# A two-layer hybrid decoder step on one core: plain products where the halves are still apart, mixtures made behind them, and two PSUM readers changed

## The chip, the core and the metric

The kernel runs on one core of a Trainium2 chip. The metric is device time in microseconds, the median over several executions. A core has five engines that run side by side, each with its own queue in order: TensorE (PE, matrix products and transposes, with its weight loads shown as PEld), VectorE (DVE), ScalarE (ACT), GpSimd (POOL) and SyncE (SP), which here issues the DMAs. Products land in PSUM; DVE and ACT read it.

## The reference

One inference step for a prompt of 1024 tokens and 8 single sample tokens, model width 1024, two layers:

```python
# layer 0: sliding-window attention, 32 query heads on 4 key/value heads of 64, window 128
q, k, v, g = split(rmsnorm(x) @ w_in_attn)
logits = where(valid, q k^T / 8 + rel_bias, -1e30)     # 128 newest keys of each query
p = exp(logits - m);  w = p / (sum(p) + exp(sink - m))
x = x + (silu(g) * (w @ v)) @ w_out_attn
# layer 1: retention, 4 heads, 256 wide keys, 512 wide values, chunks of 128
q, k, v, g = split(rmsnorm(x) @ w_in_ret);  q, k = rotary(q), rotary(k) / 16
o = ((q k^T) * decay) @ v + (q @ R) * cross;   R = decay^128 * R + (k * decay)^T @ v
x = x + (silu(g) * groupnorm(o)) @ w_out_ret
y = rmsnorm(x)
```

Also returned are the last window of keys and values and the retention states, for prompt and samples. All inputs are float32.

## The kernel before

**Numbers.** Every large float32 operand is split into a high part (a cast to the engine's `fp32r` format) and a low part (the difference). A product is three matmuls: high x high, high x low, low x high. The split of a weight tile (`wsplit`, L200 to L202) is one cast on ACT and one subtraction on POOL or DVE.

**Halves and quarters.** The 1032 tokens are two halves: half 0 has 512 prompt tokens and the 8 samples, half 1 the other 512. A half is two quarters, QT = 256 and QS = 264 columns. The activations stand transposed, with the model width over partitions in 8 blocks of 128. Blocks k and k + 4 are handled as a pair, so that with the two quarters each half is a 2 x 2 arrangement of blocks: a1, a2 (block k) and b1, b2 (block k + 4).

**Mixed jobs.** The input projections use a scheme with seven block products in place of eight. `mixtures(h, k, f)` makes, besides the plain parts of a1 (index 0), b1 (1) and b2 (6), four mixtures: sums and differences of the four blocks (indices 2 to 5). `part` writes the high and low part of one index. `mixed(wa, wb)` makes the seven weight tiles from four loaded ones by differences (`minus`, L230). `unit_job` runs seven products of 12 matmuls for each half that it handles, and adds up the results out of PSUM on DVE (`plus`, L430). A unit is two output tiles of 128 columns.

**Order.** TensorE's order is written out by hand: a `Stream` of jobs, each a generator that yields after a product, and `spread`, which calls other stages between the steps. A weight tile is prepared one tile ahead, and loaded up to three tiles before that. The other engines' instructions are ordered by the framework's planner, which also picks buffers from each pool (a tag names a group of `bufs` buffers).

**Start.** `first_load` brings pair k of a half. `first_pair` squares both blocks for the norm (ACT; summed on DVE at L289), multiplies by the gain (L1125) and calls `mixtures`. The first jobs run on one half at a time: values of half 0 (`v_unit(0)`), keys of half 0 (`k_unit(0)`), values of half 1, a turning of the values of half 0, keys of half 1, the other turning. Then come eight query and eight gate units of both halves, among which the attention stages are spread.

**Attention.** For each of 64 tiles (128 queries, 4 heads): `att_scores`, then `att_turn` transposes the probabilities into PSUM (`pt`). It makes `ptc`, the keys of the same block, as a product with a mask on DVE (L753), and `ptp`, those of the block before, by a copy on ACT (L757) and a selection on POOL (L758). `att_values` multiplies both with the values (L775). `ptc` and `ptp` have one buffer each.

**Layer boundary.** `norm(h)` makes the normalised blocks of layer 1 (L1149) and calls `mixtures`. As half 0 is ready before half 1, the two gate units (`rg_unit`) and two value units (`rv_unit`) of retention head 0 are run on half 0, then on half 1, each as a mixed job of one half; then two rotary units of both halves.

**Retention.** A chunk of 128 tokens: `ret_scores` (scores and turned keys in one PSUM tile `skt`; from it `scf`, its parts `sch` and `scl`, and the decayed keys' parts `kth` and `ktl`), `ret_turn_v`, `ret_values` (output `ro` in PSUM, state update `rp`), `group_norm` (statistics on DVE from `ro`, a power on POOL, and the scaling on ACT, L908, from `ro` into `on`), and `ret_turn`, which transposes `on` (`oT`). The PSUM tiles `skt`, `vtp`, `ro`, `oT`, `pt`, `o` and those of the sample stages share two buffers (tag `w`). In SBUF, `on`, the two tiles of the rotation and a few short rows share three (tag `s`).

Of the kernel before, what the change touches and what calls it, by code (L numbers as in the profile page):

```python
# [19 lines left out]
P = 128  # L20
# [106 lines left out]
def hybrid_step(ctx: ExitStack, tc: tile.TileContext, I: dict, O: dict):  # L127
# [171 lines left out]
    def new_h(h):  # L299
        H[h] = [[None] * 4 for _ in range(7)]  # L300

    def part(h, c, k, src, eng):

        if k % 2 == 0:
            HC[h, c, k // 2] = [htile(h, c, k // 2, n, [P, 2, QS], F32R, f"h{h}{c}{n}") for n in "hl"]
        w = src.shape[-1]
        hh, hl = [t[:, k % 2, :w] for t in HC[h, c, k // 2]]
        act.copy(hh, src)
        eng.tensor_tensor(out=hl, in0=src, in1=r32(hh), op=ALU.subtract)
        H[h][c][k] = (hh, hl)  # L310

    def mixtures(h, k, f):


        a1, a2 = f[:, 0, 0:QS], f[:, 0, QS : 2 * QS]
        b1, b2 = f[:, 1, 0:QT], f[:, 1, QS : 2 * QS]
        part(h, 0, k, a1, pool)
        part(h, 1, k, b1, vec)
        part(h, 6, k, b2, vec)
        vec.tensor_tensor(out=b2, in0=a2, in1=b2, op=ALU.add)  # L320
        pool.tensor_tensor(out=a2, in0=a1, in1=a2, op=ALU.subtract)
        vec.tensor_tensor(out=a1, in0=b2, in1=a1, op=ALU.subtract)
        part(h, 2, k, a1, vec)
        part(h, 3, k, b2, pool)
        part(h, 4, k, a2, vec)
        vec.tensor_tensor(out=b1, in0=b1, in1=a1[:, 0:QT], op=ALU.subtract)
        part(h, 5, k, b1, pool)
# [138 lines left out]

    def spill(dr, halves=(0, 1), tell=None):

        h0, nh = halves[0], len(halves)

        def done(f, q, x, psum):
            if psum:
                t = ctile(q, nh)
                act.copy(t, x)
                x = t
            if tell is not None:
                tell(f, q, x)
            sp.dma_start(dr[:, f, h0 : h0 + nh, span(q)], x)

        return done  # L480
# [76 lines left out]
    sink = cp.tile([P, HEADS], F32, name="sink")  # L557
    sink2 = cp.tile([P, HEADS], F32, name="sink2")
    nsink2 = cp.tile([P, HEADS], F32, name="nsink2")
    sink_s = cp.tile([16, 4], F32, name="sink_s")  # L560
    nsink_s = cp.tile([16, 4], F32, name="nsink_s")
# [3 lines left out]
    def bias_rows():  # L565
# [9 lines left out]
        rb = cp.tile([NBUCKET, HEADS], F32, name="rb")  # L575
# [20 lines left out]
    def k_unit(h):  # L596
        def tell(f, q, x):
# [4 lines left out]
            elif q:  # L602
                ksmp[f] = cp.tile([P, NB], F32, name=f"ksmp{f}")
                vec.tensor_copy(ksmp[f], x[:, 0, QT:QS])

        unit_job(I["w_in0"][16], I["w_in0"][17], spill(kdram, (h,), tell), (h,))
# [14 lines left out]
    def v_unit(h):  # L621
# [3 lines left out]
        def done(f, q, x, psum):  # L625
# [3 lines left out]
            act.copy(d[:, f, span(q)], x[:, 0])  # L629
# [20 lines left out]
        unit_job(I["w_in0"][18], I["w_in0"][19], done, (h,))  # L650
# [95 lines left out]
    def att_turn(i):  # L746
# [8 lines left out]
        if not first:  # L755
            ptp = lp.tile([P, 4, P], F32, name="ptp", tag="ptp", bufs=1)
            act.copy(ptp, pt)  # L757
            pool.affine_select(out=ptp, in_=ptp, pattern=[[0, 4], [-1, P]], base=-1, channel_multiplier=1, compare_op=ALU.is_ge, fill=0.0)  # L758
# [79 lines left out]
    def rg_unit(u, t, halves=(0, 1)):  # L838
        f = 32 + 4 * u + 2 * t
        unit_job(I["w_in1"][f], I["w_in1"][f + 1], spill(rgd[u][t], halves), halves)  # L840

    def rv_unit(u, t, halves=(0, 1)):
        f = 16 + 4 * u + 2 * t
        unit_job(I["w_in1"][f], I["w_in1"][f + 1], spill(rvd[u][t], halves), halves)
# [44 lines left out]
    def group_norm(o, c2, cc):  # L889
# [14 lines left out]
        on = ap_.tile([P, 512], F32, name="on", tag="s", bufs=SB)[:n]  # L904
        if cc is None:
            vec.tensor_scalar(out=on, in0=o, scalar1=r[:, 0:1], scalar2=r[:, 1:2], op0=ALU.mult, op1=ALU.add)
        else:
            act.activation(on, o, AF.Identity, bias=r[:, 1:2], scale=r[:, 0:1])  # L908
# [18 lines left out]
    def ret_scores(u, gc):  # L927
# [11 lines left out]
        vec.scalar_tensor_tensor(out=sf, in0=w[:, 0:P], scalar=kd, in1=m_le, op0=ALU.mult, op1=ALU.mult)  # L939
        sh = lp.tile([P, P], F32R, name="sch", tag="sch", bufs=1)  # L940
# [3 lines left out]
        kth = lp.tile([P, 256], F32R, name="kth", tag="kth", bufs=1)  # L944
        act.activation(kth, w[:, P : 3 * P], AF.Copy, scale=kd)
        ktl = lp.tile([P, 256], F32R, name="ktl", tag="ktl", bufs=1)
        vec.scalar_tensor_tensor(out=ktl, in0=w[:, P : 3 * P], scalar=kd, in1=r32(kth), op0=ALU.mult, op1=ALU.subtract)
# [21 lines left out]
    def ret_values(u, gc):  # L969
# [10 lines left out]
        else:  # L980
            R = lp.tile([P, 2, 512], F32, name="R", tag="R", bufs=1)
        if gc == 0:
# [8 lines left out]
        CH["on", u, gc] = group_norm(o, cst[:, C_C2 + 8 * u + gc : C_C2 + 8 * u + gc + 1], cst[:, C_CC + 8 * u + gc : C_CC + 8 * u + gc + 1])  # L991
# [12 lines left out]
    def ret_sample(u):  # L1004
# [12 lines left out]
        yield  # L1017
        tt = [sm.tile([P, 2, NB], F32, name="rrt", tag="rrt", bufs=2) for _ in range(2)]
# [9 lines left out]
        def load(i):  # L1028
            Rs, vs = [], []
            for b in (2 * i, 2 * i + 1):  # L1030
# [3 lines left out]
                for dt in range(2):  # L1034
                    R = lp.tile([P, 512], F32, name="Rsm", tag="Rsm", bufs=4)
# [76 lines left out]
    def first_load(h, k):  # L1112
        f = X0[h, k] = big("x0")
        zeros(f, h)
        src = I[f"x{h}"][k : KT : 4].rearrange("a p t -> p a t")
        sp.dma_start(f[:, :, 0:QT], src[:, :, 0:QT])
        sp.dma_start(f[:, :, QS : QS + real(h) - QT], src[:, :, QT : real(h)])

    def first_pair(h, k):
        f = X0.pop((h, k))  # L1120
        for j in range(2):
            square(f[:, j, :], 2 * QS, sums.setdefault(h, []))
        for j in range(2):
            kt = k + 4 * j
            vec.tensor_scalar(out=f[:, j, :], in0=f[:, j, :], scalar1=gcol[:, 0, kt : kt + 1], scalar2=None, op0=ALU.mult)  # L1125
        mixtures(h, k, f)
# [8 lines left out]
    def norm(h):  # L1135
# [19 lines left out]
        new_h(h)  # L1155
        for k in range(4):
            mixtures(h, k, fs[k])
# [19 lines left out]

    stream.todo[0].load()
    first_load(0, 0)
    first_load(0, 1)  # L1180
    stream.todo[1].load()
    first_load(0, 2)
    first_load(0, 3)
    stream.todo[2].load()
    for k in range(4):
        first_pair(0, k)
    sp.dma_start(cst, I["cst"])
    stream.ahead = AHEAD
    first_load(1, 0)
    first_load(1, 1)  # L1190
    bias = bias_rows()
    st = [stager(first_stats(h)) for h in range(2)]

    def pair_b(k):
        first_pair(1, k)
        if k < 2:
            first_load(1, k + 2)

    for f in (nothing, nothing, nothing, st[0], st[0], lambda: pair_b(0), lambda: next(bias), lambda: pair_b(1),
              nothing, lambda: pair_b(2), lambda: next(bias), lambda: pair_b(3)):  # L1200
        stream.step()
        f()
    stream.finish(1)
    stream.step()
    st[1]()
    stream.step()
    st[1]()
    sums.clear()
    stream.finish(4)
# [87 lines left out]
    for u in range(RH):  # L1297
        if u:
            n_head.append(jobs(rg_unit, u, 0) + jobs(rg_unit, u, 1))
        else:  # L1300
            n_b = [jobs(f, 0, t, (h,)) for h in range(2) for f in (rg_unit, rv_unit) for t in range(2)]
            n_head.append(0)
        n_head[-1] += jobs(rot_unit, 2 * u, rqd[u]) + jobs(rot_unit, 8 + 2 * u, rkd[u])
        if u:
            n_head[-1] += jobs(rv_unit, u, 0) + jobs(rv_unit, u, 1)
# [12 lines left out]
    spread(4, [stager(norm(1))] * 8 + [nothing] * 2)  # L1318
    stream.finish(4)
# [36 lines left out]
    for u in range(1, RH):  # L1356
        sm_ = [stager(ret_sample(u - 1))] * 22
# [14 lines left out]
    spread(outs1[1], mix([stager(load_y(1, 2))] * 9, chunks(29, 33), [sm_] * 12))  # L1372
# [117 lines left out]
```

## Time and profile before

| | us |
|---|---|
| median of 3 runs | 1898.75 (1896.29 to 1898.92) |
| profiled execution | 1893.53 |
| its span, first to last instruction | 1891.7 |
| PE busy | 1684.4 (89%) |
| DVE busy | 1203.1 (64%) |
| POOL busy | 915.8 (48%) |
| ACT busy | 838.9 (44%) |

Busy time is the union of an engine's instructions. A matmul's recorded duration is longer than the distance to the next one, as they overlap; where PE runs without a pause, the distance is what counts. In the rows, "L202" is a line of the kernel, "out<-in" the tiles, "x13" the count, then busy time in us and mean ns of one, and after a second bar the idle time in front of these instructions with what ended it. In a row of waits stand the waiting instruction, the one that released it, the us in total, the number of waits and the longest. A row of stretches lists, for each engine, the busy us and in brackets the instructions, then the share of its clock that TensorE was granted, and the DMA share and rate.

### The profile page before, as it was taken

How to read it: one execution, taken by the hardware profiler on the slowest of the kernel's cores; microseconds unless marked ns; L12 is line 12 of the kernel's file. 1: busy time of each engine (PE TensorE's matmuls, PEld its weight loads, DVE VectorE, ACT ScalarE, POOL GpSimd, SP SyncE). 2: the span in 40 equal slices, each digit the busy share in tenths (PEclk: the TensorE clock that was granted, in tenths of full speed). 3: DMA queues.
4: the chain of work that ended last, by engine and by line, in shares of the span. 5: the costliest groups of instructions: out<-in, count | busy, mean ns of one | idle time of the engine just before them, and what ended most of it. 6: DMA issues, size and time to landing. Idle time of an engine off the chain costs nothing. (4 is left out here: it accounts for less than half of the span.)

```text
span 1891.7 us, 32933 instructions
## 1 busy us (share of the span) xinstructions
PE 1684.4 (89%) x12072; PEld 1502.3 (79%) x12072; DVE 1203.1 (64%) x2075; ACT 838.9 (44%) x1927; POOL 915.8 (48%) x769
## 2 busy tenths in 40 slices
PE   5699998999998999987789899989998989699996
PEld 3589887788887777866789889878988879677885
DVE  7944665767667776577753676557646764767446
ACT  5544554555555454434443344334434444343223
POOL 6664454655545442335774544444544544434212
PEclk6799999999999999989899999999999999999997
DMA  4434434343435631433245565466537557664324
GB/s 141 114 116 151 147 119 127 99 130 113 126 105 174 225 106 63 154 94 103 77 135 169 169 207 168 127 201 207 175 124 217 204 189 231 219 201 140 107 68 134
DMA packets 211170, 277.99 MB, mean 147 GB/s; under 512 B 32936, under 2 KB 122656, under 8 KB 211008
## 3 DMA queue, kind: packets, MB, share of 16 engines
q1 hardware_dynamic: 211008, 275.88, 46.0%
q8 instruction: 95, 1.56, 0.3%
q14 instruction: 67, 0.55, 0.1%
HBM read 185.46 MB, written 92.42 MB: 147 GB/s over the span
## 5 line engine op out<-in xcount | busy, mean ns | idle before, releaser
L202 POOL TENSOR_TENSOR wlo<-wraw,whi 128x512 fp32r<-128x512 f32 x240 | 331.7, 1383 | 400.9 <-ACT whi L200 385.1
L200 ACT CAST whi<-wraw 128x512 fp32r<-128x512 f32 x432 | 265.3, 616 | 455.9 <-PE gemm L425 229.6
L540 PE MATMUL gemm<-yh,whi 128*128 128x260 f32 (+2 forms) x800 | 262.2, 328 | 13.9 <-DVE xf L548 13.6
L542 PE MATMUL gemm<-yh,wlo 128*128 128x260 f32 (+2 forms) x800 | 255.3, 319 | 0.0
L541 PE MATMUL gemm<-yl,whi 128*128 128x260 f32 (+2 forms) x800 | 254.4, 318 | 0.0
L202 DVE TENSOR_TENSOR wlo<-wraw,whi 128x512 fp32r<-128x512 f32 x192 | 166.3, 866 | 110.4 <-ACT whi L200 108.3
L540 PEld LDWEIGHTS gemm<-yh,whi 128*128 128x128 f32 x800 | 154.3, 193 | 37.3 <-issue 16.9
L230 POOL TENSOR_TENSOR wraw<-wraw 128x512 f32<-128x512 f32 x96 | 148.5, 1551 | 49.3 <-DVE wraw L230 35.8
L430 DVE TENSOR_TENSOR cq<-cq,gemm 128x512 f32<-128x512 f32 (+1 forms) x144 | 89.4, 621 | 119.5 <-PE gemm L426 79.8
L696 ACT ACTIVATE L<-L,nm 128x128 f32<-128x128 f32 x256 | 99.8, 391 | 144.0 <-DVE nm L691 140.1
L542 PEld LDWEIGHTS gemm<-yh,wlo 128*128 128x128 f32 x800 | 153.7, 192 | 10.1
L541 PEld LDWEIGHTS gemm<-yl,whi 128*128 128x128 f32 x800 | 154.2, 193 | 9.0
L700 POOL TENSOR_TENSOR L<-L,rsum 128x512 f32<-128x512 f32 x64 | 72.7, 1136 | 151.8 <-DVE rsum L699 65.7
L230 DVE TENSOR_TENSOR wraw<-wraw 128x512 f32<-128x512 f32 x96 | 91.0, 948 | 20.1 <-POOL wlo L202 17.0
L1054 DVE SCALAR_TENSOR_TENSOR Rsm<-vrow,ksm,Rsm 128x512 f32<-128x512 f32 x64 | 59.0, 951 | 27.3 <-ACT Rsm L1053 17.7
L545 DVE TENSOR_TENSOR xf<-xf,gemm 128x520 f32<-128x520 f32 x64 | 44.3, 692 | 48.9 <-PE gemm L542 48.8
L548 DVE TENSOR_TENSOR xf<-xf,gemm 128x512 f32<-128x512 f32 (+1 forms) x72 | 44.7, 622 | 47.3 <-PE gemm L542 47.2
L509 POOL TENSOR_TENSOR yl<-yf,yh 128x520 fp32r<-128x520 f32 (+1 forms) x32 | 44.0, 1374 | 60.8 <-ACT yh L508 60.8
L733 PE MATMUL S<-kk,q 64*128 64x256 f32 (+1 forms) x512 | 69.2, 389 | 0.1
L424 PE MATMUL gemm<-h06h,whi 128*128 128x264 f32 x168 | 52.1, 310 | 16.2 <-DVE cq L430 16.2
L677 POOL TENSOR_TENSOR g<-g,RB 128x1040 f32<-128x1040 f32 (+1 forms) x16 | 38.5, 2404 | 57.7 <-DMA g<-gd 49.7
L953 POOL TENSOR_TENSOR ql<-qk,qh 128x256 fp32r<-128x256 f32 x28 | 25.1, 897 | 84.9 <-ACT qh L951 61.6
(358 smaller groups left out, 5748.0 us busy)
## 6 DMA issues: line engine op xcount, KB each, us to landing
wraw<-in_w_in SPq DMA_DIRECT2D x192, 256.0 KB
wraw<-in_w_out SPq DMA_DIRECT2D x96, 256.0 KB
ydram<-y SPq DMA_DIRECT2D x32, 512.0 KB
Rsm<-in_state SPq DMA_DIRECT2D x64, 256.0 KB
out_ret_state_sample<-Rsm SPq DMA_DIRECT2D x64, 256.0 KB
yf<-ydram SPq DMA_DIRECT2D x32, 260.0 KB
yf<-ydram SPq DMA_DIRECT2D x32, 256.0 KB
v<-rv SPq DMA_DIRECT2D x32, 256.0 KB
```

The costliest lines, as they stand in the source:

```text
L200: act.copy(hi, raw)
L202: eng.tensor_tensor(out=lo, in0=raw, in1=r32(hi), op=ALU.subtract)
L230: eng.tensor_tensor(out=out, in0=x, in1=y, op=ALU.subtract)
L424: pe.matmul(o, wh, hh, start=(first and k == 0), stop=False, skip_group_check=not first)
L430: vec.tensor_tensor(out=x, in0=x, in1=ps, op=ALU.add)
L540: pe.matmul(ps, a, yh[:, c0:c1], start=(k == 0), stop=False)
L541: pe.matmul(ps, a, yl[:, c0:c1], start=False, stop=False)
L542: pe.matmul(ps, b, yh[:, c0:c1], start=False, stop=(k == 3))
L696: act.activation(L[:, i, :], L[:, i, :], AF.Exp, bias=nm[:, i : i + 1], accum_out=rs[:, i : i + 1])
L700: pool.tensor_tensor(out=L, in0=L, in1=rs[:, :, None].to_broadcast([n, nh, P]), op=ALU.mult)
L733: pe.matmul(S[:, 2 * par + j, w0:256], q[r, j, cs], kk[r, (gb - 1) * P + w0 : (gb + 1) * P], start=True, stop=True)
L1054: vec.scalar_tensor_tensor(out=R, in0=vs[j // 2], scalar=ksm[:, dt, b : b + 1], in1=R, op0=ALU.mult, op1=ALU.add)
```

## The change

1. **Plain jobs.** `plain_job` runs all eight block products of one half: four weight tiles as they are loaded, 96 matmuls, sums kept in PSUM, one copy out per result. Keys and values of both halves and the two gate units of retention head 0 use it. It needs a fourth plain part, of a2 (index 7), whose parts get buffers that are free at that time (`home`).
2. **Value units of head 0** are run on both halves at once, as mixed jobs, after the rotary units.
3. **`mixtures` is split** into `plain_parts` (four plain parts) and `mixture` (the four mixed ones), and the calls are moved: plain parts first, mixtures between later steps. At the start the plain parts come straight from the loaded block with the gain folded in: the high part by an ACT activation with a scale, the low part by a DVE instruction for each. Squares and the gain on the whole block follow. `first_load` takes one block in place of two. In layer 1, block 0's and block 1's low parts are on DVE, those of 6 and 7 on POOL.
4. **`ptp`** is `pt - ptc`, one DVE instruction.
5. **`ret_scores`** issues `kth` and `ktl` ahead of `sch` and `scl`. **`ret_values`** copies `ro` to SBUF on ACT (`on`), and the group norm reads and scales that copy in place.
6. The sample generator of retention has one more empty stage; small tiles move to other pools, and `Rsm` is a little larger.

```diff
-    def mixtures(h, k, f):
-        a1, a2 = f[:, 0, 0:QS], f[:, 0, QS : 2 * QS]
-        b1, b2 = f[:, 1, 0:QT], f[:, 1, QS : 2 * QS]
-        part(h, 0, k, a1, pool)
-        part(h, 1, k, b1, vec)
-        part(h, 6, k, b2, vec)
+    def plain_parts(h, k, j, f, home, gains=None):
+        a, b = parts(f)[2 * j : 2 * j + 2]
+        g = None if gains is None else gains(k + 4 * j)
+        part(h, j, k, a, vec, g)
+        if j:
+            part(h, 6, k, b, pool, g)
+        else:
+            part(h, 7, k, b[:, 0 : QT if h else QS], pool, g, home)
+    def mixture(h, k, f):
+        a1, a2, b1, b2 = parts(f)
...
+            act.activation(hh, src, AF.Copy, scale=gain)
+            vec.scalar_tensor_tensor(out=hl, in0=src, scalar=gain, in1=r32(hh), op0=ALU.mult, op1=ALU.subtract)
...
+    def plain_job(wa, wb, done, h):
+        def run():
+            hs = H[h]
+            gs = [gtile(), gtile()]
+            ns = [QT, QT if h else QS]
+            for z in range(2):
+                for f in range(2):
+                    hi, lo = stream.tile()
+                    for q, n in enumerate(ns):
+                        o = gs[f][:, q, :n]
+                        for k in range(4):
+                            hh, hl = [x[:, :n] for x in hs[(0, 7, 1, 6)[2 * z + q]][k]]
+                            wh, wl = hi[:, k * P : (k + 1) * P], lo[:, k * P : (k + 1) * P]
+                            pe.matmul(o, wh, hh, start=(z == 0 and k == 0), stop=False)
+                            pe.matmul(o, wh, hl, start=False, stop=False)
+                            pe.matmul(o, wl, hh, start=False, stop=(z == 1 and k == 3))
+                    if z:
+                        for q, n in enumerate(ns):
+                            done(f, q, gs[f][:, q : q + 1, :n], True)
+                    yield 24 * mm_ns(QS)
...
-            act.copy(ptp, pt)
-            pool.affine_select(out=ptp, in_=ptp, pattern=[[0, 4], [-1, P]], base=-1, channel_multiplier=1, compare_op=ALU.is_ge, fill=0.0)
+            vec.tensor_tensor(out=ptp, in0=pt, in1=ptc, op=ALU.subtract)
...
+        on = ap_.tile([P, 512], F32, name="on", tag="s", bufs=SB)
+        act.copy(on, o)
...
-        CH["on", u, gc] = group_norm(o, ...)
+        CH["on", u, gc] = group_norm(on, ...)
...
     for k in range(4):
-        first_pair(0, k)
+        first_load(0, k, 0)
+        stream.todo[k].load()
+    for k in range(4):
+        first_load(0, k, 1)
+    first_parts(0, 0)
+    stream.step()
+    stream.ahead = AHEAD
+    first_parts(0, 1)
+    stream.step()
     sp.dma_start(cst, I["cst"])
+    first_squares(0, 0)
+    stream.step()
...
+    first_squares(0, 1)
+    stream.finish(1)
...
+    for k in range(4):
+        stream.step()
+        if k < 2:
+            st[0]()
+        mixture(0, k, X0[0, k])
...
-    spread(4, [stager(norm(1))] * 8 + [nothing] * 2)
-    stream.finish(4)
+    nb = stager(norm(1))
+    spread(2, [nb] * 6 + [na] * 2)
+    spread(2, [nb] * 4)
     stream.finish(n_head[0])
```

176 lines of the change are left out of this document (108 added, 68 removed).

## The prediction

> **What bounds the kernel now.** I read the totals first, then a table of busy time over stretches that I cut at the kernel's own stages, then TensorE's waits (PE) stage by stage, then the costliest lines of the other engines inside the stages where PE waits. PE is busy 89% of the span, so the question is where the rest lies.
>
> ```profile
> PE 1684.4 (89%) x12072; PEld 1502.3 (79%) x12072; DVE 1203.1 (64%) x2075; ACT 838.9 (44%) x1927; POOL 915.8 (48%) x769
> ```
>
> The cuts come from the first matmul of the first two-half job of layer 0 (118.08), the first matmul of layer 1 (881.21) and the first two-half job of layer 1 (1000.38):
>
> ```profile
> 118.08 0.57 PE L424 MATMUL gemm<-h00h,whi 128*128 128x264 f32 x1
> ```
> ```profile
> 881.21 0.57 PE L424 MATMUL gemm<-h00h,whi 128*128 128x264 f32 x1
> ```
> ```profile
> 1000.38 0.29 PE L424 MATMUL gemm<-h00h,whi 128*128 128x264 f32 x1
> ```
> ```profile
> core 0: us, PE busy (x) PEld busy (x) DVE busy (x) ACT busy (x) POOL busy (x), PEclk, DMA share, GB/s
> 7.70:118.00 110.30, 66.92 (x381) 57.35 (x381) 91.28 (x147) 57.98 (x135) 75.08 (x65) 0.75 0.40 116
> 118.00:700.00 582.00, 548.22 (x4231) 474.83 (x4231) 375.96 (x728) 292.39 (x826) 297.43 (x244) 0.98 0.43 136
> 700.00:881.00 181.00, 166.08 (x1059) 138.12 (x1058) 120.31 (x220) 77.14 (x200) 69.98 (x76) 0.97 0.34 107
> 881.00:1000.30 119.30, 95.53 (x676) 91.50 (x677) 75.30 (x108) 53.87 (x117) 86.42 (x63) 0.89 0.33 103
> 1000.30:1590.00 589.70, 544.38 (x4077) 509.80 (x4077) 357.64 (x572) 250.50 (x457) 286.76 (x225) 0.98 0.56 179
> 1590.00:1840.00 250.00, 224.97 (x1427) 195.69 (x1425) 150.26 (x236) 85.15 (x148) 83.08 (x69) 0.98 0.51 164
> 125.00:150.00 25.00, 25.00 (x209) 25.00 (x209) 10.60 (x15) 8.05 (x14) 12.14 (x9) 1.00 0.40 128
> ```
>
> The last row gives PE's own speed in these jobs: 209 matmuls in 25 us, 0.12 us each. Two stages fall far below it. In the start (keys and values of both halves) 381 matmuls take 110 us, where 0.12 each would be 46, while DVE is busy 91 of the 110. At the head of layer 1, 676 take 119 us, where 81 would do, and there POOL is the busiest helper (86 of 119). Attention (118 to 700) and retention (1000 to 1840) are PE-bound with 34 and 70 us of gaps. Only a shorter start or head, or a removed gap, can shorten the span; elsewhere the helpers' savings are hidden under PE.
>
> **The start: plain products for K and V.** A single-half mixed job has 7 weight tiles and 84 matmuls, a plain one 4 tiles and 96. PE's own work grows by 4 x 12 x 0.12 = 5.8 us. What the helpers lose and gain is priced by these rows of the first 118 us:
>
> ```profile
> L202 DVE TENSOR_TENSOR wlo<-wraw,whi 128x512 fp32r<-128x512 f32 x13 | 12.3, 945 | 11.2 <-ACT whi L200 11.1
> L230 DVE TENSOR_TENSOR wraw<-wraw 128x512 f32<-128x512 f32 x10 | 10.4, 1042 | 0.9 <-DMA wraw<-in_w_in 0.6 <-POOL wlo L202 0.2
> ...
> L430 DVE TENSOR_TENSOR cq<-cq,gemm 128x256 f32<-128x256 f32 (+1 forms) x12 | 5.0, 415 | 5.1 <-PE gemm L426 5.1
> ...
> L309 DVE TENSOR_TENSOR h16l<-x,h16h 128x264 fp32r<-128x264 f32 x4 | 3.3, 827 | 0.0
> ```
> ```profile
> L202 POOL TENSOR_TENSOR wlo<-wraw,whi 128x512 fp32r<-128x512 f32 x18 | 25.9, 1442 | 15.1 <-ACT whi L200 14.0 <-PE bps L581 1.0
> L230 POOL TENSOR_TENSOR wraw<-wraw 128x512 f32<-128x512 f32 x10 | 15.8, 1584 | 5.7 <-DVE wraw L230 3.0 <-DMA wraw<-in_w_in 2.7
> ...
> L309 POOL TENSOR_TENSOR h10l<-x,h10h 128x264 fp32r<-128x264 f32 x4 | 3.8, 942 | 2.8 <-ACT h10h L308 2.8
> ```
>
> DVE loses, per job, two weight differences and one split, and over the four jobs twelve sums out of PSUM: 8 x 1.042 + 4 x 0.945 + 12 x 0.415 = 17.1 us. It gains the low parts: before 16 plain ones were on DVE (blocks 1 and 6) and 8 on POOL (block 0); now all 32 (blocks 0, 1, 6 and the new 7) are DVE instructions with the gain folded in. 16 more at 0.827, the row of the nearest, are 13.2. DVE goes from 91.3 to 87.4. POOL loses 8 x 1.584 + 8 x 1.442 + 8 x 0.942 = 31.7 and falls from 75 to 43. ACT loses 12 weight casts and gains 8 part casts, and is no bound (58 of 110).
>
> So DVE's work hardly shrinks. Two things move. DVE's prices here are swollen by POOL: the same 128x256-to-264 subtraction takes 0.41 us alone and about 0.98 beside a POOL one, while a DVE instruction with an operand in PSUM keeps 0.67 in the middle of one:
>
> ```profile
> 843.59 0.98 DVE L322 TENSOR_TENSOR xn<-xn 128x264 f32<-128x264 f32 x1
> ...
> 849.02 0.41 DVE L326 TENSOR_TENSOR xn<-xn 128x256 f32<-128x256 f32 x1
> ...
> 851.14 0.67 DVE L548 TENSOR_TENSOR xf<-xf,gemm 128x512 f32<-128x512 f32 x1
> ```
> ```profile
> 850.93 0.91 POOL L309 TENSOR_TENSOR h00l<-xn,h00h 128x264 fp32r<-128x264 f32 x1
> ```
>
> With POOL busy 32 us less I take 82 for DVE. And PE no longer sits behind the mixtures: values and keys of half 0 need only its 16 plain parts, so the matmuls run while DVE makes squares and mixtures, and PE's tail after DVE's last mixture shrinks. I lay it out as 6 us of loading, about 70 us of DVE until the sums of half 1 exist (all but half 1's four mixtures, 20 instructions at 0.4 to 0.8, some 12 us), then on PE the turning of both halves' values (about 8 us with its waits on ACT) and the last key job (96 x 0.12 = 11.5), together 96: the first two-half job starts at 96 where it was 118. Gain 22. Lower end: DVE at 87.4 with no price falling, from 7.7 on, and a tail of 20 behind it gives 115, gain 3; if the 13 us of new parts simply add, minus 13. Upper end: PE alone, 429 matmuls at 0.12 behind 12 us of loads and half-speed warm-up, gives 64 and a gain of 54; the nearer row is DVE's, so I stay low. The 16 more, half-sized x loads add 16 issues of 0.47 on SP (its rows at 1.72 to 5.83, the one below) in a queue that only feeds the same DMAs; DMA is at 0.40 here and I give it nothing.
>
> ```profile
> 2.19 0.47 SPq L1117 DMA_DIRECT2D x<-in_x  x1
> ```
>
> [...]
>
> **The head of layer 1.** Two gate units become plain per half, two value units go back to both halves at once. PE: 8 x 84 = 672 matmuls become 4 x 96 + 2 x 168 = 720, 86.4 us at 0.12. Weight tiles: 56 become 16 + 14 = 30; 8 weight loads of 256 KB go. PE's waits there are:
>
> ```profile
> PE gemm L424 <- DVE cq L430: 8.6, 2, 7.9
> PE gemm L426 <- POOL wlo L202: 8.3, 6, 3.0
> ```
>
> A mixed single-half job costs POOL 4 x 1.442 + 2 x 1.584 = 8.9 us per 84 x 0.12 = 10.1 us of PE: POOL is nearly the pace. Plain costs it 2 x 1.442 per 11.5. The POOL wait goes. The DVE one is the second half's norm (16 instructions in a block around 890 to 900, ahead of everything else on DVE); that block stays, and the plain jobs' DVE weight splits will queue behind it, so I keep 13 of lost time (8 of wait and some 5 of half-clock restart; the granted clock was 0.89 in this stage). 86.4 + 13 is about 100 against 119.3: gain 19. Ends: 8 if the gates of half 1 wait for their parts too, 28 if half the loss goes.
>
> **Attention: second tile as a difference.** Removed per tile: an ACT copy and a POOL selection; added: one DVE subtraction of the shape of the first tile's product.
>
> ```profile
> L753 DVE TENSOR_TENSOR ptc<-pt,cst 128x512 f32<-128x512 f32 x64 | 43.8, 684 | 12.1 <-PE pt L751 11.9
> L758 POOL TENSOR_SCALAR_AFFINE_SELECT ptp<-ptp 128x512 f32<-128x512 f32 x56 | 39.8, 711 | 29.7 <-ACT ptp L757 29.6
> L757 ACT COPY ptp<-pt 128x512 f32<-128x512 f32 x56 | 32.7, 583 | 32.5 <-DVE ptc L753 23.7 <-DVE nm L691 4.8 <-POOL L L700 2.6
> ```
> ```profile
> PE o L775 <- POOL ptp L758: 26.6, 16, 6.2
> PE pt L751 <- POOL L L700: 5.4, 3, 3.5
> ```
>
> The chain is product on DVE, copy on ACT, selection on POOL, and PE waits for its end 16 times. The tile made first, on DVE from the same PSUM, never appears among PE's waits, and the subtraction stands next to it. DVE gains 56 x 0.684 = 38 us: 376 becomes 414 of 582, 71%, not the pace. Behind it queue the max, sums and weight splits; they slip by 0.7 once per slot of about 9 us of PE. I take 24 of the 26.6. Ends: 32 (POOL's relief also removes the 5.4), and minus 12 (every subtraction lands on PE's path: 26.6 - 38).
>
> **Retention: ro copied out, kth before sch.** Waits of PE from 1000 to 1840:
>
> ```profile
> PE vtp L962 <- DVE ktl L947: 9.3, 6, 3.5
> PE oT L914 <- ACT on L908: 7.8, 3, 4.2
> PE oT L914 <- DVE ktl L947: 6.9, 3, 4.6
> PE osum L1072 <- ACT on L908: 6.1, 2, 3.5
> ...
> PE og L1060 <- DVE ktl L947: 3.9, 1, 3.9
> PE vtp L962 <- ACT on L908: 3.4, 5, 1.2
> ```
> ```profile
> L892 DVE BATCH_NORM_STATS2 bst<-ro x32: 683/699/702, 1072.3 to 1760.7; 128x6 f32<-128x512 f32 x32
> L908 ACT ACTIVATE on<-ro,gr x32: 767/779/786, 1077.1 to 1765.1; 128x512 f32<-128x512 f32 x32
> ```
>
> ro holds one of two PSUM buffers from the statistics to the scaling, 4.8 us in the first chunk (1072.3 to 1077.1). With the copy (an ACT copy of 128x512 out of PSUM was 0.583) the buffer is free in about a quarter of that: of 6.1 + 3.4 I take 7. The oT waits on `on` are for the data itself, and the copy stands ahead of it: 3 x 1 us worse. ktl no longer stands behind the casting and subtraction of the scores, about 0.9 us (an estimate: the two neighbouring steps of 256 columns are under 0.5 each): 10 waits x 0.9 = 9 of 20.1. The copies add 32 x 0.583 = 19 us to an ACT that is busy 336 of 840; 1 us. Together 12. Ends: minus 10 (no buffer wait goes, oT waits in more chunks) and 30 (all go). The reordering of tiles between pools, the extra empty stage of the sample generator and the larger Rsm tile issue nothing; their cover is PE, and without it they would cost a few short instructions' delay.
>
> **Sum.** 22 + 19 + 24 + 12 = 77. The profiled execution took 1893.5 us (its span is 1891.7), so 1816.5 there; the median of the runs, 1898.75, lies 5.2 above it, so 1822.
>
> **Rivals.**
> (a) The waits move instead of going: the DVE subtraction is late in its queue, and oT waits for the copied ro. For it: DVE reaches 71%. Against: the first tile's product, same queue, makes PE wait for nothing. Attention then gives 6, retention 2: 22 + 19 + 6 + 2 = 49, 1850.
> (b) More goes than I credit: POOL's relief unswells DVE everywhere. Start 40, head 28, attention 32, retention 22: 122, 1777. For it: the 0.41 against 0.98. Against: norm and mixtures remain.
> (c) Slower: `on` now takes one of three shared SBUF buffers (tag s) from the copy on, 4.8 us longer per chunk, and the rotation takes two of them, the sample's row one. If the buffers run out, ro cannot be copied and PE stands. At the full 4.8 in 32 chunks this costs 154 against 65 from the other places: 1988. It decides from 2.0 us per chunk (65 / 32). Against it: a chunk's `on` is turned before the next one is made, and rotation comes every second chunk.
> (d) No change: a denser PE is granted less clock. 4% less of 1684 would eat 70 of the 77. Against: the clock was 1.00 in the 25 us in which PE never paused.
>
> **How the numbers follow.** Forecast 0.58, (a) 0.18, (b) 0.10, (c) 0.08, (d) 0.06. Faster by over 0.2% (about what a measurement of this kernel can tell): 0.86; within it 0.06; slower 0.08. The range reaches past (a), to 1868, and half-way to (b), to 1785; (c), (d) and the rest of (b) are left out, 0.2. The forecast's own range is 1800 to 1845.
>
> **What would show it.** Right: the first two-half job near 96 us; layer 1's head about 100 us long; no PE wait on the second tile, and its DVE row at about 0.68; no PE wait on the group norm except oT's; ktl's waits halved. Wrong: PE waits with DVE's subtraction as releaser, DVE near 90% in attention, the copy of ro waiting for a buffer, or a start whose last mixtures still end past 90 us.

## The result, and the profile after

The changed kernel took 1830.79 us in the median of 3 runs (1828.01 to 1835.26) against 1898.75: a ratio of 0.9649 with a 95% interval of 0.9616 to 0.9682, 68 us less. 1822 was forecast, with a range of 1785 to 1868. The profiled execution took 1835.26 (span 1833.4), 58 less than the one before. The rest of the 68 is that the profiled execution of before lay 5 below its median and this one 4 above.

The totals of the page, and the same table of busy time over stretches as in the prediction, cut at the first two-half job of layer 0 (95.1), the norm of layer 1's first half (788.3), layer 1's first matmul (853.4), the end of the head (952.7) and the first retention chunk (1010.6):

```profile
PE 1675.0 (91%) x12168; PEld 1505.2 (82%) x12168; DVE 1173.1 (64%) x2083; ACT 806.8 (44%) x1867; POOL 815.7 (44%) x669
```
```profile
core 0: us, PE busy (x) PEld busy (x) DVE busy (x) ACT busy (x) POOL busy (x), PEclk, DMA share, GB/s
6.10:95.10 89.00, 64.91 (x431) 57.67 (x431) 73.51 (x137) 51.88 (x126) 52.67 (x46) 0.85 0.54 153
95.10:788.30 693.20, 658.38 (x5074) 572.84 (x5074) 467.03 (x922) 312.07 (x912) 296.18 (x233) 0.98 0.42 132
788.30:853.40 65.10, 53.17 (x214) 41.47 (x214) 49.42 (x78) 27.26 (x58) 30.81 (x33) 0.90 0.34 103
853.40:952.70 99.30, 92.43 (x724) 91.09 (x725) 48.12 (x71) 41.54 (x91) 48.68 (x42) 0.95 0.36 109
952.70:1010.60 57.90, 54.36 (x434) 53.94 (x434) 20.77 (x29) 18.80 (x33) 26.64 (x20) 0.97 0.50 152
1010.60:1781.90 771.30, 713.93 (x5058) 653.24 (x5056) 481.64 (x778) 333.63 (x604) 344.89 (x272) 0.97 0.56 178
```

The stages of three profiled executions, each cut at the same instructions (us; "again" is the unaltered changed kernel in a later run, below):

| stage | before | after | after, again | after less before | forecast |
|---|---|---|---|---|---|
| start, up to the first two-half job | 118.1 | 95.1 | 96.1 | -23 | -22 |
| attention, up to the norm of layer 1 | 698.1 | 693.2 | 691.9 | -5 | -24 |
| layer boundary | 65.0 | 65.2 | 63.7 | 0 | 0 |
| layer 1 up to the first chunk | 175.4 | 157.2 | 156.3 | -18 | -19 |
| retention, up to the final norm | 781.6 | 771.3 | 769.0 | -10 | -12 |
| final norm, up to its last matmul | 46.0 | 44.2 | 44.5 | -2 | 0 |

The end of the head in the changed kernel is set where about the prediction's 720 matmuls are done; its last jobs there are rotary units, not value units. Three of the four terms came out near their forecast; attention gave 5 of 24. PE's largest wait in attention before, over the whole stage (the 26.6 of the prediction ends at 700), then PE's largest waits there in the changed kernel, and the rows of the two instructions that end them:

```profile
PE o L775 <- POOL ptp L758: 27.2, 17, 6.2
```
```profile
PE pt L794 <- POOL L L743: 15.4, 5, 6.4
PE o L817 <- DVE ptp L800: 7.1, 7, 2.4
```
```profile
L743 POOL TENSOR_TENSOR L<-L,rsum 128x512 f32<-128x512 f32 x64 | 71.0, 1110 | 155.3 <-DVE rsum L742 84.3 <-ACT whi L200 30.8 <-ACT cq L515 14.1
```
```profile
L800 DVE TENSOR_TENSOR ptp<-pt,ptc 128x512 f32<-128x512 f32 x56 | 38.4, 686 | 0.5
```

The wait for the second tile fell from 27.2 to 7.1 as its chain of two engines became one DVE instruction. But the wait for the probabilities themselves (L743, where the softmax divides its rows by their sums) grew from 5.4 to 15.4. PE's time outside its busy time went from 698.1 - 660.3 = 37.8 to 34.8; its busy row of before in that stage:

```profile
118.10:816.20 698.10, 660.33 (x5073) 571.00 (x5073) 446.17 (x867) 344.51 (x972) 337.06 (x289) 0.98 0.42 132
```

PE's waits in retention, from 912 to 1782:

```profile
PE oT L960 <- ACT on L954: 42.2, 12, 9.7
PE gemm L441 <- DVE cq L447: 7.9, 4, 2.8
...
PE og L1109 <- DVE ktl L989: 1.1, 1, 1.1
PE oT L960 <- DVE ktl L989: 0.8, 1, 0.8
```

The waits for `ktl` fell from 20.1 to 2, and those for a PSUM buffer held by the group norm (9.5) are gone. In their place PE waits 42.2 us, was 7.8, for the group norm's data at the turning of a chunk. These three together wait 7 us longer than before (37 before, 44 after). That the stage is still 10 shorter comes from PE's other waits in it, which fell from 29 to 10; the largest of those before were

```profile
PE vsp L1042 <- DMA vsm<-rv: 6.0, 1, 6.0
...
PE vtp L962 <- issue: 5.3, 2, 2.7
PE rp L886 <- DVE vl L966: 4.1, 3, 2.1
```

None of the three is among PE's waits after. `vsm` is a row of the samples, loaded in the stage of the sample generator behind which the change puts an empty one; no run tries that by itself.

### The profile page after: what moved, and what is told of

The parts are those of the page before. It is cut to its first block, busy times and chain, and to the rows that moved or that the text cites. A ratio compares the mean times of both kernels' runs of the same rounds, so it can differ in the third digit from the quotient of the medians.

```text
span 1833.4 us, 32913 instructions
## 1 busy us (share of the span) xinstructions
PE 1675.0 (91%) x12168; PEld 1505.2 (82%) x12168; DVE 1173.1 (64%) x2083; ACT 806.8 (44%) x1867; POOL 815.7 (44%) x669
## 5 line engine op out<-in xcount | busy, mean ns | idle before, releaser
L202 POOL TENSOR_TENSOR wlo<-wraw,whi 128x512 fp32r<-128x512 f32 x216 | 294.9, 1366 | 487.8 <-ACT whi L200 463.6
L200 ACT CAST whi<-wraw 128x512 fp32r<-128x512 f32 x394 | 242.0, 616 | 462.6 <-PE gemm L442 219.2
L202 DVE TENSOR_TENSOR wlo<-wraw,whi 128x512 fp32r<-128x512 f32 x178 | 145.2, 816 | 116.1 <-ACT whi L200 114.8
L584 PEld LDWEIGHTS gemm<-yh,wlo 128*128 128x128 f32 x800 | 154.8, 193 | 10.4
L743 POOL TENSOR_TENSOR L<-L,rsum 128x512 f32<-128x512 f32 x64 | 71.0, 1110 | 155.3 <-DVE rsum L742 84.3
L447 DVE TENSOR_TENSOR cq<-cq,gemm 128x512 f32<-128x512 f32 (+1 forms) x114 | 78.4, 688 | 87.3 <-PE gemm L443 49.9
L230 POOL TENSOR_TENSOR wraw<-wraw 128x512 f32<-128x512 f32 x76 | 107.6, 1416 | 43.1 <-DVE wraw L230 38.4
L230 DVE TENSOR_TENSOR wraw<-wraw 128x512 f32<-128x512 f32 x76 | 67.9, 893 | 26.9 <-POOL wlo L202 25.2
L550 ACT CAST yh<-yf 128x520 fp32r<-128x520 f32 (+1 forms) x64 | 39.5, 623 | 70.1 <-DMA yf<-ydram 61.2
L960 PE MATMUL oT<-cst,on 128*128 128x128 f32 x128 | 22.8, 307 | 44.7 <-ACT on L954 42.2
```

The source lines that it names most:

```text
L200: act.copy(hi, raw)
L202: eng.tensor_tensor(out=lo, in0=raw, in1=r32(hi), op=ALU.subtract)
L230: eng.tensor_tensor(out=out, in0=x, in1=y, op=ALU.subtract)
L447: vec.tensor_tensor(out=x, in0=x, in1=ps, op=ALU.add)
L584: pe.matmul(ps, b, yh[:, c0:c1], start=False, stop=(k == 3))
L743: pool.tensor_tensor(out=L, in0=L, in1=rs[:, :, None].to_broadcast([n, nh, P]), op=ALU.mult)
```

## The experiments

All were timed against the kernel before on the same chip. The unaltered changed kernel was run once more beside the last three.

**The changed kernel again.**

> The changed kernel again, unaltered, on the chip of the other runs of this call: it gives the direct comparison for the kernel with both edits, and a second profile by which to read how far a stage of one profile differs from that of another without any edit. Expected: 1827 to 1836, ratio 0.962 to 0.968; stages within 3 us (start, head) and within 8 us (attention, retention) of the first profile's. If the stages lie closer than that, differences of 5 us between kernels' profiles can be read as effects; if further apart, none of that size can.

Measured: 1830.29 us, ratio 0.9653 (0.9626 to 0.9680). The stages (table above) lie within 2.3 us of the first profile's. But a stage also moves when an edit is made elsewhere. Over the runs below that leave a stage alone, the start is 94.7 to 96.5 long, attention 688.4 to 695.0, layer 1 up to the first chunk 154.4 to 160.8, and retention 764.3 to 778.9. Only what lies outside these ranges is read as an effect. The intervals of the ratios below reach 0.23 to 0.53% to either side.

**The start: is it the weight work?** Two runs. The first turns back the written order, for both halves alike (half 0 is shown), and keeps the plain jobs:

```diff
     first_parts(0, 0)
+    first_parts(0, 1)
+    first_squares(0, 0)
+    first_squares(0, 1)
+    for k in range(4):
+        mixture(0, k, X0[0, k])
     stream.step()
...
```

> The changed kernel with the start's order turned back: plain key and value jobs as changed, but all parts, squares, gains and the four mixtures of a half ahead of that half's first product. Theory O (the order carries the gain: PE ran from 14 us on because it needed only the plain parts): the first two-half job starts 10 to 20 us later than 95, and the time rises by as much, to 1841 to 1851. Theory W (the smaller weight work carries it, 16 tiles for 28): under 5 us later.

Measured: 1834.39 us, ratio 0.9651 (0.9610 to 0.9692), start 95.6. DVE's order of instructions hardly differed from that of the changed kernel (it reads the squared sums of half 1 at 74.6, against 74.5): the planner sorts the helper engines' work itself. So the order in which the calls are written carries none of the 23 us, but whether the plain jobs gain by less weight work or by needing only plain parts was not told apart. The second run leaves the jobs and adds weight work whose results go nowhere: 28 instructions of 128x512 on DVE and POOL, as many as the change took away, but 16 on DVE and 12 on POOL where the change had taken 12 and 16 (n counts the four weight tiles of a job, raw is the loaded tile):

```diff
+    def extra(n, raw):
+        if n < 3:
+            hi = lp.tile([P, 4, P], F32R, name="xhi", tag="bias", bufs=2).rearrange("p a b -> p (a b)")
+            act.copy(hi, raw)
+            lo = lp.tile([P, 4, P], F32R, name="xlo", tag="bias", bufs=2).rearrange("p a b -> p (a b)")
+            (pool, vec, vec)[n].tensor_tensor(out=lo, in0=raw, in1=r32(hi), op=ALU.subtract)
+        eng = pool if n % 2 else vec
+        t = lp.tile([P, 4, P], F32, name="xm", tag="ptp", bufs=1).rearrange("p a b -> p (a b)")
+        eng.tensor_tensor(out=t, in0=raw, in1=raw, op=ALU.subtract)
...
```

> The changed kernel, but each of the start's four plain jobs (keys and values of a half) also does the weight work that it was relieved of: per job 3 more copies on ACT with their 3 subtractions (2 on DVE, 1 on POOL) and 4 more subtractions of whole weight tiles (2 on DVE, 2 on POOL). Their outcomes go nowhere. In all 12 ACT, 16 DVE and 12 POOL instructions of 128x512. TensorE's own work and its order stay. Theory W (the start's 23 us are the weight work, by load on DVE and POOL): at the rows of the start before the change (0.945 a split on DVE, 1.45 to 1.58 on POOL) 16 DVE make 15 us and 12 POOL 18 us, and the prices of the remaining rows go back up with them, so that the start goes from 95 to 110 to 118 and the whole to 1845 to 1855. Theory O (the start gained because plain products need none of the mixtures, so TensorE starts and goes on without them, and the helper engines have room for the rest): the start stays at 95 to 99, the whole at 1828 to 1836.

Measured: 1849.83 us, ratio 0.9757 (0.9724 to 0.9789), start 115.9: 20.8 us of the 23 are lost again. Busy time of this run over the changed kernel's start, the columns as above, then DVE's instruction that reads the squared sums of half 1 (`rs<-nps`) in the kernel before, in the changed kernel, and in this run:

```profile
6.10:95.10 89.00, 51.06 (x315) 46.44 (x316) 86.78 (x142) 52.84 (x120) 58.48 (x54) 0.74 0.40 117
```
```profile
84.48 0.14 DVE L262 TENSOR_SCALAR rs<-nps 128x4 f32<-128x4 f32 x1
```
```profile
74.48 0.15 DVE L262 TENSOR_SCALAR rs<-nps 128x4 f32<-128x4 f32 x1
```
```profile
94.86 0.15 DVE L275 TENSOR_SCALAR rs<-nps 128x4 f32<-128x4 f32 x1
```

DVE is busy 86.8 of 89 us here, against 73.5, and the norm of half 1 comes 20.4 us later, as much as the stage itself. PE waits for it: the largest of its waits in this start is

```profile
PE nps L273 <- DVE sqs L302: 18.8, 2, 10.8
```

So the start ends some 21 us behind DVE's block of parts, squares and mixtures in the changed kernel and in this run, and weight work pushes that block apart. The times of theory W came in, but this run does not bring the start of before back: its block ends 10.4 us later than the one of before, for DVE has the new low parts and four more weight instructions than it had there (though not the twelve sums out of PSUM). What PE does behind the block is the other part. From the norm of half 1 to the first two-half job, before, after and in this run:

```profile
84.50:118.10 33.60, 23.59 (x167) 21.28 (x167) 19.33 (x28) 16.66 (x37) 23.58 (x16) 0.90 0.44 130
```
```profile
74.50:95.10 20.60, 17.21 (x115) 14.31 (x115) 8.82 (x14) 7.84 (x19) 7.67 (x6) 0.87 0.78 202
```
```profile
94.90:115.90 21.00, 17.90 (x117) 14.91 (x117) 6.51 (x14) 7.74 (x18) 6.65 (x5) 0.83 0.65 166
```

Before, PE still had 60 matmuls of the values of half 1 and all 84 of its keys to do at that point; with plain jobs the values of half 1 are done by then, and 96 matmuls of the keys are left. So the 23 us are 10 by which DVE's block ends earlier and 13 by which PE's tail is shorter, and the tail stays short when the weight work is there. Neither theory holds alone. No run separates the weight work from the other savings in the 10.

**The head of layer 1 as mixed jobs.** The gate units become mixed again, the value units of head 0 are run one half at a time again, the mixtures of half 0 are called ahead of these jobs, and the norm of half 1 beside four of them in place of two.

```diff
 def rg_unit(u, t, h=None):
-            plain_job(I["w_in1"][f], I["w_in1"][f + 1], spill(rgd[u][t], (h,)), h)
+            unit_job(I["w_in1"][f], I["w_in1"][f + 1], spill(rgd[u][t], (h,)), (h,))
...
-    spread(2, [nb] * 6 + [na] * 2)
-    spread(2, [nb] * 4)
+    spread(4, [nb] * 10 + [nothing] * 2)
+    stream.finish(4)
```

> The changed kernel with the head of layer 1 as before: the two gate and two value units of head 0 as mixed jobs of one half each, and the mixtures of half 0 ahead of them. If the head's gain of 18 us comes from the plain jobs and the two-half value units, the time rises by 15 to 22 us, to about 1849, and the head stands at about 117 us again. If it comes from the earlier stages' moved mixtures or from a shift of other work, it rises by less than 6.

Measured: 1857.42 us, ratio 0.9785 (0.9732 to 0.9838). The head is 117.0 long again, where 99.3 stands above, and layer 1 up to the first chunk is 179.2, 22 more:

```profile
854.00:971.00 117.00, 92.35 (x676) 88.73 (x676) 75.83 (x108) 54.01 (x117) 82.73 (x62) 0.90 0.34 107
```
```profile
PE gemm L441 <- DVE cq L447: 8.0, 1, 8.0
PE gemm L443 <- POOL wlo L202: 6.4, 6, 1.1
PE gemm L443 <- DVE wlo L202: 5.5, 1, 5.5
```

POOL is busy 83 us against 49, and PE waits for weight tiles from POOL, DVE and ACT. The plain jobs, with the moves of the value units and of the mixtures that go with them, account for the whole of this stage's gain; the run does not tell these three apart. Retention is 778.9 in this profile, the longest of all the runs that leave it alone.

**The second tile: by itself, and undone.** In the changed kernel undone (the two lines with minus and plus changed about), and in the kernel before alone:

```diff
-            act.copy(ptp, pt)
-            pool.affine_select(out=ptp, in_=ptp, pattern=[[0, 4], [-1, P]], base=-1, channel_multiplier=1, compare_op=ALU.is_ge, fill=0.0)
+            vec.tensor_tensor(out=ptp, in0=pt, in1=ptc, op=ALU.subtract)
```

> The changed kernel with the second probability tile made as before (ACT copy, POOL selection); all else as changed. Theory M (the waits moved: in attention PE now waits for POOL's normalisation and the subtraction together about as long as it waited for the selection): the time rises by 3 to 8 us, to about 1836, and the attention stage, 693 us from the first two-half job to the norm of layer 1's half 0, goes back to about 698. Theory P (the subtraction is worth the 24 us that were predicted, and another part of the change costs attention 20): the time rises by about 24, to 1855.

> The kernel before with the subtraction alone. Theory M: 3 to 8 us faster than before, about 1893, with PE's waits for the selection (27 us) replaced by waits for POOL's normalisation, for the subtraction and for the gated product, 20 to 30 us together. Theory P: about 24 us faster, 1875, and no such waits.

Measured: undone 1846.37 us, ratio 0.9727 (0.9683 to 0.9771), attention 700.5; alone 1900.88, ratio 1.0002 (0.9979 to 1.0025), attention 701.2. PE's waits in attention of the kernel before with the subtraction alone:

```profile
PE pt L751 <- POOL L L700: 17.7, 6, 6.7
PE o L774 <- DVE ptp L757: 7.9, 7, 2.2
```

By itself the subtraction trades 27 us of one wait for 12 more of the other (5.4 before, 17.7 here), 8 of its own and several small ones, and gains nothing. Undone it costs 0.8%, 15 us in the medians, between the 3 to 8 and the 24 of the two theories; the profile shows 7 us of it, in attention. There the waits are 25.7 for the selection and 6.7 for the division, so in both kernels the second grows when the first goes. Why the edit is worth 7 us in one and nothing in the other stays open.

**Where the attention's gain went.** Two runs on L743. First the division is moved from POOL to DVE, then it is left out.

```diff
-        pool.tensor_tensor(out=L, in0=L, in1=rs[:, :, None].to_broadcast([n, nh, P]), op=ALU.mult)
+        vec.tensor_tensor(out=L, in0=L, in1=rs[:, :, None].to_broadcast([n, nh, P]), op=ALU.mult)
```

> The changed kernel with the softmax's normalisation (128x512, 64 times) on DVE in place of POOL. Theory M with POOL's queue as the holder (gating and key scaling of 2.4 us stand ahead of the normalisation): the 15 us of PE's waits for it go, and the time falls by 8 to 14 us, to about 1820. Theory D (DVE's queue is the holder, since POOL was idle 84 us for the reciprocal): DVE gains another 44 us, waits appear behind DVE instead, and the time is the same or up to 8 us worse.

> The changed kernel without the softmax's normalisation at all (64 POOL instructions of 1.11 us with 71 us busy, and 4 for the sample; the output is then not divided by the row sums; the sums themselves are still made). In the attention TensorE waits 15.4 us for that instruction, the largest of its waits there. Theory D (every link of the softmax's chain is about equally late: maximum and its minimum on DVE, four exponentials on ACT, the second tile's subtraction on DVE): the wait for the normalisation goes and others of some 10 us come in its place, attention 686 to 693, the whole 1823 to 1833. Rival (POOL's normalisation is the one link that took the gain forecast for the attention): attention 670 to 676, the 24 us forecast less the 5 that came, the whole 1808 to 1815.

Measured on DVE: 1831.13 us, ratio 0.9640, attention 689.9. Left out: 1816.41 (1812.02 to 1819.22), ratio 0.9584 (0.9547 to 0.9621), attention 666.6. The busy rows of attention, first with the division on DVE, then without it:

```profile
95.30:785.20 689.90, 657.69 (x5073) 571.27 (x5073) 503.20 (x990) 312.05 (x912) 225.83 (x165) 0.98 0.42 132
```
```profile
95.50:762.10 666.60, 653.04 (x5073) 567.95 (x5073) 454.29 (x922) 311.69 (x912) 222.61 (x165) 0.99 0.44 137
```

and PE's largest waits there, first with the division on DVE, then without it:

```profile
PE pt L794 <- DVE nm L734: 6.4, 1, 6.4
PE pt L794 <- DVE es L736: 6.0, 1, 6.0
PE o L817 <- DVE ptp L800: 5.6, 7, 1.6
```
```profile
PE o L816 <- DVE ptp L799: 3.3, 6, 0.7
PE pt L793 <- ACT ptb L853: 2.7, 1, 2.7
```

In both POOL has some 70 to 74 us less to do. Moved, PE's time outside its busy time is 32.2, against 34.8, and attention stays within the range of unedited runs. The two longest waits are put down to a maximum and to the sink's term on DVE; both end within 0.2 us of the end of a division there. Left out, that time falls to 13.6, and no other wait takes the place. Leaving the division out takes more than its own time out of the chain from a tile's scores to its turning: only the division needs the row sums, the sink's exponential and the reciprocal, so the turning no longer waits for these either. So relieving POOL by itself does not help, and not every link of the chain is equally late, as theory D had it: the waits hang on the division and what comes ahead of it for its sake. How much of them is the division's own 1 us, and whether POOL's queue held it back where DVE's does now, is not told apart.

Attention is 26.6 us shorter, about the 24 of the forecast; 21 of them are PE's idle time, the rest its busy time. The whole gained less, 14 us in the medians and 17 to 21 in the profiles; layer 1 up to the first chunk is 160.8 in that profile, 4 longer.

**Retention: the copy, the order, and a later turning.** `ro` read in place without the copy; `sch` and `scl` issued ahead of `kth` and `ktl` as before; and `ret_turn` of a chunk put behind the next chunk's output product.

```diff
-        on = ap_.tile([P, 512], F32, name="on", tag="s", bufs=SB)
-        act.copy(on, o)
...
-            on = o
-            act.activation(o, o, AF.Identity, bias=r[:, 1:2], scale=r[:, 0:1])
+            on = ap_.tile([P, 512], F32, name="on", tag="s", bufs=SB)[:n]
+            act.activation(on, o, AF.Identity, bias=r[:, 1:2], scale=r[:, 0:1])
...
```
```diff
-            out = [v, t] + out if gc == 0 else [v] + out + [t]
+            def v():
+                ret_values(*divmod(j - 1, 8))
+                while late:
+                    ret_turn(*late.pop(0))
+                late.append(divmod(j - 1, 8))
+                if j == 32:
+                    ret_turn(*late.pop(0))
+            out = [v] + out
```

> The changed kernel, with the group norm reading ro from PSUM as before, without the copy. Theory A (the copy frees PSUM but lets the group norm's chain slip behind other work, and PE's waits for turning on, 42 us after the change against 8 before, eat most of the gain): about the same, within 6 us of 1831, with waits for on of 10 to 15 us back as buffer waits. Theory B (the copy is worth the whole 10 us of the retention stage): 8 to 12 us slower, about 1841.

> The changed kernel with the scores' parts ahead of the keys' parts again. Theory A: with ro copied out the PSUM buffers no longer hang on ktl, so PE's waits for ktl stay under 5 us and the time within 4 us of 1831. Theory B (the order was what removed the 20 us of ktl waits): 6 to 10 us slower, with those waits back.

> The changed kernel with each chunk's turning of on moved on PE from the end of the next chunk's scores and values to after the next chunk's output product. Theory A (42 us of PE waits are only the order on PE, which comes before a chain of eight steps has ended): those waits fall under 8 us and the time falls by 20 to 35, to about 1803. Theory S (on then holds one of three shared SBUF buffers for a chunk longer, and rotation or the copy of ro waits for one): waits appear behind the copy of ro or the rotation, and the time is within 6 us of 1831 or above.

Measured: without the copy 1838.23 us, ratio 0.9681 (0.9643 to 0.9719), retention 776.8; old order 1833.67, 0.9645 (0.9616 to 0.9673), 773.1; late turning 1831.82, 0.9651 (0.9611 to 0.9690), 761.3. PE's waits in retention without the copy, then with the old order, then with the late turning:

```profile
PE oT L960 <- ACT on L954: 11.8, 4, 4.7
PE skt L981 <- DVE oacc L1112: 8.5, 3, 4.9
PE oT L960 <- DVE vl L1012: 7.1, 4, 2.7
PE gemm L441 <- DVE cq L447: 6.7, 4, 2.6
PE vtp L1008 <- ACT on L954: 5.2, 2, 3.2
```
```profile
PE oT L960 <- ACT on L954: 42.6, 12, 10.5
```
```profile
PE gemm L441 <- DVE cq L447: 12.1, 6, 3.5
PE oT L960 <- ACT on L954: 7.8, 1, 7.8
PE gemm L582 <- DVE xf L590: 7.0, 3, 4.1
PE skt L981 <- ACT on L1029: 6.3, 4, 4.2
```

The copy makes the long waits at the turning (11.8 without it, 42 with it) and takes away smaller ones: PE's time outside its busy time is 56 us without it and 57 with it. The medians put its worth at some 5 to 8 us, with intervals that overlap; the stage's 776.8 lies within the range of runs that leave retention alone, so the profile does not show it. The order of the keys' parts is worth nothing that shows, and the waits for `ktl` stay at 3 us in both runs, so that neither edit alone took them away; what did is open. The late turning ends the 42 us, but others come up; the stage is 3 us shorter than the shortest unedited one, the first chunk begins 3 us later than in the changed kernel, and nothing is left in the median.

**The two edits that looked best together.**

> The changed kernel with the softmax's normalisation on DVE in place of POOL and the retention's turning of a chunk's output put on TensorE behind the next chunk's output product, the two edits run singly before. Their profiles gave attention 689.9 and retention 761 to 764 against 693.2 and 771.3 with medians level with the changed kernel's. Theory A (each edit only hands its wait to the next late link): 1826 to 1834, ratio 0.962 to 0.966. Rival (the profiled stages' gains are real, hidden in the spread of the medians, and add): 1815 to 1822, ratio 0.956 to 0.959.

Measured: 1832.87 us, ratio 0.9668 (0.9642 to 0.9694), attention 694.0, retention 761.0. They do not add up to anything: no version that computes the whole was measurably faster than the changed kernel.

## Why the prediction was right, and where it was not

The forecast of 1822 was 9 us too low. By the stages of the profiled executions 19 us are missing, all of them in attention; the medians lie 68 apart and the profiles 58, so that the total looks closer than its parts.

- **Start (22 forecast, 23 measured): right, by the mechanism too.** The layout had the squared sums of half 1 at 76 and a tail of 20 on PE behind them; they came at 74.5, and the tail was 20.6. Both reasons given count: DVE's block ended 10 us earlier, and PE's tail shrank by 13. DVE was busy 73.5 us, not 82. The term mis-sized was the 16 new low parts, put at 13.2: all 32 took 17.9 (0.56 each) where the 16 of before took 12.1, so that they added 5.8. The gain's multiplication, which the sum left as it was, went from 13.5 to 8.7 as well. POOL did not fall to 43 but to 52.7.
- **Head (19 forecast, 18 measured): right.** 99.3 us long against "about 100", and mixed jobs in the same place bring 117 back. The waits for POOL's weight tiles (8.3) went. The 13 of lost time are 12.4 (99.3 less 724 matmuls at 0.12). The wait for DVE's block shows, as forecast, as one for a weight split (4.2).
- **Attention (24 forecast, 5 measured): the step that failed.** The subtraction's own price (0.684 forecast, 0.686 measured) and DVE's share (467 of 693 us, 67%) were right. But the 7.1 us in 7 waits for the subtraction are one of the signs that the prediction had named for being wrong. What failed is the step that 24 of 26.6 us of a wait would go because its releaser did. The profile of before had the next link in the same list, `pt` on `L`, with 5.4. That was read as the most that could still be lost there. It was what the second tile's wait had left uncovered: with the subtraction alone in the kernel before, it grew to 17.7. This is rival (a)'s figure of 6 for attention, by another mechanism than its late DVE queue.
- **Retention (12 forecast, 10 measured): right in size by luck.** "No wait on the group norm except the turning's" held, but the turning's grew by 34 us where "3 x 1 us worse" stood; here rival (a), "oT waits for the copied ro", saw what came. The `ktl` waits went nearly to nothing instead of by half, though not by the reordering alone. The waits that the forecast named add up to 7 us more, not 12 less. The 10 come from waits that it had left alone (29 before, 10 after), and the empty stage of the sample generator, put at nothing, may be part of that.
- **Rivals.** (b) is out: no stage gave what it asks, though DVE's prices did fall. (c) is out: retention became no longer, and PE waits 0.3 us in all for a copy of `ro`. (d) is out: the granted clock was 0.960 over the whole, against 0.953.

## What to carry to other kernels

A wait in the list is not the gain of removing its releaser: look for the next wait on the same engine in the same loop, and ask how long that link's chain is, for its row shows only what the first wait leaves uncovered. Leaving a step out, beside a run that only moves it, shows whether relieving its engine is enough; but with a step goes all that only it waits for, so such a run prices the chain ahead of the step as well. Where a stage is bound by a helper engine, trading that engine's work for more matmuls pays. Giving the work back with unused results shows whether the stage follows that engine; how much each part of a change was worth is read by cutting the stage where the engine's block ends, not by how much of the gain is lost again.

## What the runs showed of the hardware

A DVE instruction can be held up by POOL although it reads a single tile. The multiplication of a block by its gain (128x528, one tile and one column of scalars), in the kernel before, the changed kernel, and the changed kernel with the weight work added, each with the shortest, median and longest of 16 in ns:

```profile
L1125 DVE TENSOR_SCALAR x<-x,gcol x16: 479/916/1529, 6.8 to 68.5; 128x528 f32<-128x528 f32 x16
```
```profile
L1193 DVE TENSOR_SCALAR x<-x,gcol x16: 477/483/1499, 5.3 to 58.0; 128x528 f32<-128x528 f32 x16
```
```profile
L1206 DVE TENSOR_SCALAR x<-x,gcol x16: 474/484/1615, 6.3 to 80.0; 128x528 f32<-128x528 f32 x16
```

The floor is 0.48 us in all three. In these profiles 16 of the 48 took over 0.8 us (9, 1 and 6 of them). Each of the 16 began while POOL was at a subtraction of two tiles, and ended about 0.29 us behind POOL's end (one 0.38, with two short POOL writes between); the other 32 took 0.47 to 0.50, even where such a POOL instruction began while they ran. One of the 16, with the POOL instruction beside it:

```profile
68.51 1.50 DVE L1125 TENSOR_SCALAR x<-x,gcol 128x528 f32<-128x528 f32 x1
```
```profile
68.35 1.38 POOL L202 TENSOR_TENSOR wlo<-wraw,whi 128x512 fp32r<-128x512 f32 x1 [0.99 <-PE bps L581]
```

The prediction had only the subtractions of two tiles down as swollen. The granted clock of the start went with PE's busy share: 0.75 before (61% busy), 0.85 after (73%), and 0.74 over the same 89 us with the weight work added (57%).
